# A mixture-of-experts trunk on one core: the first pair of experts of each layer started one product ahead, copied by one engine and worked in halves

## The chip, the core and the metric

The kernel runs on one core of a Trainium2 chip. A core has a matrix engine (TensorE, PE in the rows; its weight loads are the rows PEld), a vector engine (DVE), a scalar engine (ScalarE, ACT), GpSimd (POOL), a queue engine that issues most transfers (SyncE, SP), and 16 DMA engines that move data between the memory of the chip and the core's on-chip memory. TensorE writes its products to accumulation banks, from which ScalarE and the vector engine read them.

The metric is the device time of one execution in microseconds. A kernel is timed in several runs, and the median counts. One further execution is recorded by the hardware profiler; its rows are quoted below.

## What is computed

Two decoder layers over 256 tokens of width 1024. Each layer is a token mixer (a gated linear recurrence in layer 0, a stick-breaking attention in layer 1, both beside a cross-attention into a memory) and a two-level mixture of experts, each followed by a residual and a layer norm. The change is in the mixture of experts:

```python
def hier_moe(x, w_group, b_group, w_router, b_router, w_gate, w_up, w_down):
    probs_g = jax.nn.softmax((xf @ w_group + b_group), axis=-1)
    p_top, g_idx = lax.top_k(probs_g, 1)
    logits_e = (xf @ w_router + b_router).reshape(T, N_GROUPS, EXPERTS_PER_GROUP)
    in_group = jnp.take_along_axis(logits_e, g_idx[:, :, None], axis=1)[:, 0]
    probs_in = jax.nn.softmax(in_group, axis=-1)
    w_top, e_local = lax.top_k(probs_in, TOP_K_IN_GROUP)
    w_top = w_top / jnp.sum(w_top, axis=-1, keepdims=True)
    ...
    h = jax.nn.silu(jnp.einsum('td,edf->tef', xf, w_gate)) * jnp.einsum('td,edf->tef', xf, w_up)
    y = jnp.einsum('tef,efd->td', h * gates[:, :, None], w_down)
```

There are 16 experts with 256 inner features each; every token goes to two of them. The products with the experts' weights are in 32-bit floats.

## The kernel before

**Tiling.** The experts are worked in eight pairs, p = 0 to 7. Each expert has 64 slots for tokens, so that a pair fills 128 columns of inputs. For a pair, the rows of the tokens in its slots are brought together (features in partitions, tile `xg` for even and `ex` for odd p), multiplied with the gate and up weights into one accumulation bank `gu` (the two experts in the two halves of the partitions; gate columns 0 to 255, up columns 256 to 511), put through Silu and multiplied (`h`, lines L871 to L876), transposed (`ht`, copied to `hT`, L895 to L900), and multiplied with the down weights into two banks `po` of 512 output columns each (L908 to L925). A gate and up step over one block of 128 features is two products of 64 rows by 512 columns, one for each expert; eight such blocks k = 0 to 7 make the sum. A program product shows as two records of half its work, and those of the two experts of a pair run side by side.

**Weights.** All weights stream through SyncE's queue as tiles of 1 MB, `w` in the rows (line L94). Six tiles belong to a pair: four for gate and up, two for down. A ring of buffers holds them; a tile's transfer starts when its buffer is free and when the transfer three tiles before it has landed. `stream.done` gives buffers back.

**The head of a mixture.** At the end of the mixer (`mixer_end`, L937 to L1092) the second half of the tokens (t = 1) is normed while its features are transposed into the router's input: `turn_in` (L561 to L567) makes four transposes into one bank `zt` and lets ScalarE copy it to `sT`; `logits` (L569 to L574) multiplies with the router's weights. From the ranks come one-hot matrices of the slots: `P0` for the first pair, `P1` for all. The first pair's rows are gathered by products with `P0` (`gather_first`, L635 to L645, into `xgp`), the later pairs' by a DMA with computed indices: `indices` (L653 to L670) makes 16 small products of one column (tile `idx`) and starts the fetches of pairs 1 and 2 on GpSimd. `first_rows` (L647 to L651) applies the norm's scale and shift to the gathered rows, blocks 0 to 3 by ScalarE and 4 to 7 by the vector engine. `gates` (L696 to L728) works out the gate values on the vector engine and, with two products `tot`, the largest count of tokens of an expert.

**The order.** Up to the end of `mixer_end`'s routing, the order on DVE, PE and ACT is that of the code (`manual_schedule`). Behind it (L1069 onward: `moe.indices`, `moe.first_rows`, `moe.run`) instructions in `pin(...)` keep the order of the code on their engine, and a scheduler places the rest.

**The first pair in `run`** (L803 to L934): `gu(0, range(4))` multiplies blocks 0 to 3, then `gates` and `turn(0)` (two small products `ptp` that turn the gates into the order of slots), then blocks 4 to 7. Silu and the product with up follow in two parts of 128 features (`parts`), the two transposes `ht`, the first `po` bank (L913), the eight transposes `xgp` of the next pair's rows (L791), and the second `po` bank; pair 1's products come next. `hr` is the copy of `po` on its way out.

## Time and profile before

| | |
|---|---|
| median of three runs | 525.6 us (524.14 to 529.12) |
| the profiled execution, its own time | 526.96 us |
| its span in the trace | 525.3 us |
| busy: PE | 491.1 us (93%) |
| busy: PEld | 326.7 us (62%) |
| busy: DVE | 300.2 us (57%) |
| busy: ACT | 229.6 us (44%) |
| busy: POOL | 62.9 us (12%) |
| moved by DMA | 161.61 MB, mean 308 GB/s |

The two mixtures of experts lie at about 166 to 278 us (layer 0) and 408 to 512 us (layer 1). A row of the timeline has the start in us from the span's start, the duration in us, the engine, the line of the program, the operation, the tiles (out<-in), the shapes, and `x` with the number of instructions that were merged into the row; in brackets stands how long the engine was idle before it, and what released it. A q behind an engine's name is its sequencer or queue. Ends of TensorE's products are modelled, and a merged row lasts to the end of its last instruction, which can overlap the next row.

### The profile page before, as it was taken

The numbers are of one execution on the slowest core, as the hardware profiler recorded it, in microseconds if no ns is written. First come the engines' busy times: TensorE is split into PE (matmuls) and PEld (weight loads), VectorE is DVE, ScalarE is ACT, GpSimd is POOL, SyncE is SP. The second block draws the span as 40 slices with busy tenths as digits, with TensorE's granted clock in tenths as the row PEclk, the third lists the DMA queues.
The fourth block names the chain that finished last, engine by engine and source line by source line (L and its number), as shares of the span: only waits on it lengthen the run. The fifth ranks groups of instructions, "written<-read, shape, count | busy, mean of one in ns | idle before, by whom it ended". The sixth has DMA issues, their size and how long they took to land. (4 is left out here: it accounts for less than half of the span.)

```text
span 525.3 us, 9096 instructions
## 1 busy us (share of the span) xinstructions
PE 491.1 (93%) x3534; PEld 326.7 (62%) x3534; DVE 300.2 (57%) x682; ACT 229.6 (44%) x471; POOL 62.9 (12%) x78
## 2 busy tenths in 40 slices
PE   4999999999999999999797999998998899999992
PEld 4998898788996333333236889877687333333431
DVE  4668876867758622233338698677445842233547
ACT  4845446684445222333017566668423232222322
POOL 1100000002132111112011500000010121111201
PEclk9999999999999999999898999999998999999997
DMA  8999834447888999999999763242999799999922
GB/s 270 407 404 404 345 103 160 161 156 326 299 332 321 384 403 384 394 385 407 409 379 395 271 252 143 100 160 99 381 365 364 288 382 419 414 422 409 412 119 81
DMA packets 28439, 161.61 MB, mean 308 GB/s; under 512 B 5239, under 2 KB 5623, under 8 KB 11363
## 3 DMA queue, kind: packets, MB, share of 16 engines
q1 hardware_dynamic: 20736, 140.76, 68.3%
q0 software_dynamic: 4752, 10.94, 5.4%
q10 hardware_dynamic: 2902, 9.26, 4.8%
q8 instruction: 30, 0.49, 0.4%
q14 instruction: 19, 0.16, 0.1%
HBM read 158.92 MB, written 13.64 MB: 329 GB/s over the span
## 5 line engine op out<-in xcount | busy, mean ns | idle before, releaser
L820 PE MATMUL gu<-w,ex 128*64 128x512 f32 x256 | 62.9, 609 | 3.4 <-DMA w<-in_w_all_dram 2.3
L820 PE MATMUL gu<-w,xg 128*64 128x512 f32 x256 | 60.8, 601 | 0.1
L913 PE MATMUL po<-w,hT 128*64 128x512 f32 (+1 forms) x272 | 58.4, 570 | 0.1
L913 PEld LDWEIGHTS po<-w,hT 128*64 128x64 f32 x272 | 18.8, 136 | 34.0 <-issue 27.3
L820 PEld LDWEIGHTS gu<-w,ex 128*64 128x64 f32 x256 | 17.2, 137 | 34.8 <-issue 26.1
L820 PEld LDWEIGHTS gu<-w,xg 128*64 128x64 f32 x256 | 16.4, 136 | 26.5 <-issue 24.6
L920 DVE COPY hr<-po 128x512 f32<-128x512 f32 x10 | 6.9, 692 | 43.1 <-PE po L913 43.0
L629 ACT ACTIVATE xg<-xgp,lnT 128x128 f32<-128x128 f32 x32 | 13.5, 457 | 25.6 <-PE xgp L791 22.4
L918 DVE TENSOR_TENSOR hl<-po,hl 128x512 fp32r<-128x512 f32 (+1 forms) x14 | 8.5, 615 | 26.5 <-ACT hl L917 25.5
L627 DVE TENSOR_SCALAR xg<-xgp,lnT 128x128 f32<-128x128 f32 x32 | 12.4, 408 | 19.0 <-ACT xg L629 15.7
L629 ACT ACTIVATE ex<-xgp,lnT 128x128 f32<-128x128 f32 x32 | 14.3, 458 | 19.3 <-PE xgp L791 19.0
L627 DVE TENSOR_SCALAR ex<-xgp,lnT 128x128 f32<-128x128 f32 x32 | 13.1, 410 | 15.1 <-ACT ex L629 13.9
L900 ACT ACTIVATE hT<-ht 128x256 f32<-128x256 f32 (+1 forms) x18 | 6.5, 360 | 34.4 <-PE ht L899 34.3
L873 ACT ACTIVATE h<-gu 128x256 f32<-128x256 f32 (+1 forms) x18 | 6.3, 360 | 34.3 <-PE gu L820 34.3
L234 DVE TENSOR_TENSOR wo<-w,wo 128x512 fp32r<-128x512 f32 x20 | 13.7, 727 | 10.8 <-ACT wo L226 10.8
L760 POOL DMA_INDIRECT hd<-hr,own x10 | 10.1, 1014 | 81.2 <-DVE gsl L780 76.3
L673 POOL DMA_INDIRECT zg<-zd,idx x14 | 14.6, 1041 | 43.2 <-PE xgp L791 25.1
L791 PEld LDWEIGHTS xgp<-cst,zg 128*128 128x128 f32 x112 | 12.0, 141 | 11.4 <-PE gu L820 7.3
L1291 POOL TENSOR_TENSOR rms<-rms,neghalf 128x2 f32<-128x2 f32 x6 | 4.1, 699 | 111.6 <-ACT sq L1287 99.4
L384 POOL PARTITION_BROADCAST gbm<-gbm x4 | 5.3, 1398 | 94.2 <-DMA gbm<-in_ln_dram 85.5
L226 ACT ACTIVATE wo<-w 128x512 fp32r<-128x512 f32 x20 | 11.5, 628 | 9.8 <-PE wo L472 8.2
L917 ACT ACTIVATE hl<-po 128x512 fp32r<-128x512 f32 (+1 forms) x14 | 7.5, 537 | 18.4 <-PE po L913 18.4
(462 smaller groups left out, 1357.7 us busy)
## 6 DMA issues: line engine op xcount, KB each, us to landing
w<-in_w_all_dram SPq DMA_DIRECT2D x131, 1024.0 KB
hd<-in_w_all_dram ACTq DMA_DIRECT2D x2, 2560.0 KB
w<-in_w_all_dram SPq DMA_DIRECT2D x6, 256.0 KB
x_tok<-in_x_tok_dram ACTq DMA_DIRECT2D x1, 1024.0 KB
zd<-z ACTq DMA_DIRECT2D x2, 512.0 KB
gbo<-in_ln_dram ACTq DMA_DIRECT2D x1, 1024.0 KB
out_dram<-z SPq DMA_DIRECT2D x4, 256.0 KB
w<-in_w_all_dram SPq DMA_DIRECT2D x1, 512.0 KB
```

The costliest lines, as they stand in the source:

```text
L226: self.last_hi = nc.scalar.activation(p[:, 0, s], src[:, s], AF.Copy, scale=1.0 if scale is None else scale).ins
L234: nc.vector.tensor_sub(p[:, 1, s], src[:, s], p[:, 0, s])
L627: ins = nc.vector.tensor_scalar(xg[:, kk], ps, g, b, op0=ALU.mult, op1=ALU.add)
L629: nc.scalar.activation(xg[:, kk], ps, AF.Identity, scale=g, bias=b)
L673: nc.gpsimd.indirect_dma_start(out=self.zg[:, p % 2], out_offset=None, in_=self.zd, in_offset=bass.IndirectOffsetOnAxis(ap=self.idx[:, p:p ...
L760: pin(nc.gpsimd.indirect_dma_start(out=self.hd, out_offset=bass.IndirectOffsetOnAxis(ap=self.own[:, p:p + 1], axis=0), in_=src, in_offset= ...
L791: pin(nc.tensor.transpose(ps[:, k], self.zg[:, p % 2, (4 * hk + k) * P:(4 * hk + k + 1) * P], ident))
L820: pin(nc.tensor.matmul(gus[p][c * 64:(c + 1) * 64], xgs[p][:, kk, c * CAP:(c + 1) * CAP], ws[p][2 * kh + c][0][:, k * 512:(k + 1) * 512], ...
L913: pin(nc.tensor.matmul(po[c * 64:(c + 1) * 64], hT[:, f, c * 64:(c + 1) * 64], ws[p][4 + c][0][:, f * D + s.start:f * D + s.stop], start=( ...
L917: self.hl_last = nc.scalar.activation(hl[:, 0, s], po, AF.Copy).ins
L918: pin(nc.vector.tensor_sub(hl[:, 1, s], po, hl[:, 0, s]))
L920: nc.vector.tensor_copy(hr[:, p % 2, s], po)
```

## The change

1. `turn_in`: for t = 1 and the second half of the features (hk = 1) the copy to `sT` is made in two parts of 256 columns, each after two of the four transposes.
2. `first_rows`: all eight blocks of the first pair are made by ScalarE (`features(..., 0)`).
3. `indices` is called in `run`, behind the first block's products `gu(0, range(1))`, and its 16 products are pinned there; blocks 1 to 3 and `gates` follow. The two products `tot` are not pinned.
4. Pair 0's gate and up columns are put in another order in the bank: first gate and up of inner features 0 to 127, then gate and up of 128 to 255. Blocks 0 to 3 are multiplied in whole width; blocks 4 to 7 once for the first half of 256 columns and then once for the second, which makes 16 products of 256 columns from 8 of 512. Silu and the product with up read the halves.
5. Pair 0's down products: for the first 128 inner features into both `po` banks as soon as the first part of `hT` is there, then the transpose of the second part, then the second 128 features for the first bank, the next pair's eight transposes, and the second 128 features for the second bank.

The same code serves both layers.

```diff
--- before.py
+++ after.py
@@ -562,9 +562,12 @@
 
             ps = bank(f"zt{self.l}", tag="y", shape=(P, 4, P))
             sT = self.sT[t, hk] = self.tmp.tile([P, 4, P], F32, tag="sT", name=f"sT{self.l}{t}", bufs=2)
+
+            n = 2 if t == hk == 1 else 4
             for k in range(4):
                 nc.tensor.transpose(ps[:, k], s[:, t, (4 * hk + k) * P:(4 * hk + k + 1) * P], ident)
-            nc.scalar.activation(sT, ps, AF.Copy)
+                if k % n == n - 1:
+                    nc.scalar.activation(sT[:, k + 1 - n:k + 1], ps[:, k + 1 - n:k + 1], AF.Copy)
 
         def logits(self, t, hk):
             if hk == 0:
@@ -647,7 +650,7 @@
         def first_rows(self):
             xg = self.work.tile([P, NK, P], F32, tag="xg", name=f"xg{self.l}")
             for k in range(NK):
-                self.features(xg, self.first[k // 4][:, k % 4], k, k // 4)
+                self.features(xg, self.first[k // 4][:, k % 4], k, 0)
             return xg
 
         def indices(self):
@@ -658,8 +661,8 @@
             ps = bank(f"idx{l}", tag="m", shape=(P, 8))
             for p in range(8):
                 for t in range(NT):
-                    nc.tensor.matmul(ps[:, p:p + 1], self.P1f[:, t, p * P:(p + 1) * P], tokb[:, t:t + 1], start=(t == 0),
-                                     stop=(t == 1))
+                    pin(nc.tensor.matmul(ps[:, p:p + 1], self.P1f[:, t, p * P:(p + 1) * P], tokb[:, t:t + 1],
+                                         start=(t == 0), stop=(t == 1)))
 
 
             pin(nc.vector.tensor_scalar(self.idx[:, 0:3], ps[:, 0:3], float(T), T - 1.0, op0=ALU.add, op1=ALU.min))
@@ -809,7 +812,7 @@
 
             quarters = [slice(0, 512), slice(512, 768), slice(768, D)]
 
-            def gu(p, ks):
+            def gu(p, ks, part=slice(0, 512)):
 
                 if p not in ws:
                     ws[p] = [stream.get() for _ in range(6)]
@@ -817,10 +820,13 @@
                 for kk in ks:
                     kh, k = kk // 4, kk % 4
                     for c in range(2):
-                        pin(nc.tensor.matmul(gus[p][c * 64:(c + 1) * 64], xgs[p][:, kk, c * CAP:(c + 1) * CAP],
-                                            ws[p][2 * kh + c][0][:, k * 512:(k + 1) * 512], start=(kk == 0),
-                                            stop=(kk == NK - 1)))
-                    if k == 3:
+                        w = ws[p][2 * kh + c][0][:, k * 512:(k + 1) * 512]
+                        if p == 0:
+                            w = w.rearrange("p (g h n) -> p h g n", g=2, h=2)
+                            w = w if part.stop - part.start == 512 else w[:, part.start // 256]
+                        pin(nc.tensor.matmul(gus[p][c * 64:(c + 1) * 64, part], xgs[p][:, kk, c * CAP:(c + 1) * CAP],
+                                            w, start=(kk == 0), stop=(kk == NK - 1), skip_group_check=(p == 0)))
+                    if k == 3 and part.stop == 512:
                         stream.done(ws[p][2 * kh][1], ws[p][2 * kh + 1][1])
 
             def combine(p, t, s):
@@ -835,10 +841,13 @@
 
             for p in range(8):
                 if p == 0:
-                    gu(0, range(4))
+                    gu(0, range(1))
+                    self.indices()
+                    gu(0, range(1, 4))
                     self.gates()
                     self.turn(0)
-                    gu(0, range(4, 8))
+                    for j in range(2):
+                        gu(0, range(4, 8), slice(256 * j, 256 * j + 256))
                     self.ex = slots.tile([P, 2, D], F32, tag="ex", name=f"ex{l}")
                 else:
 
@@ -869,11 +878,14 @@
                 h = pool.tile([P, 256], F32, name=f"h{l}")
 
                 parts = [slice(0, 256)] if p else [slice(0, P), slice(P, 256)]
-                for c in parts:
-                    nc.scalar.activation(h[:, c], gus[p][:, c], AF.Silu)
-                for c in parts:
-                    pin(nc.vector.scalar_tensor_tensor(h[:, c], gus[p][:, 256 + c.start:256 + c.stop],
-                                                       self.gsl[:, p:p + 1], h[:, c], op0=ALU.mult, op1=ALU.mult))
+
+                g = [c.start * (1 if p else 2) for c in parts]
+                n = 256 // len(parts)
+                for c, o in zip(parts, g):
+                    nc.scalar.activation(h[:, c], gus[p][:, o:o + n], AF.Silu)
+                for c, o in zip(parts, g):
+                    pin(nc.vector.scalar_tensor_tensor(h[:, c], gus[p][:, o + n:o + 2 * n], self.gsl[:, p:p + 1], h[:, c],
+                                                       op0=ALU.mult, op1=ALU.mult))
                 if p == 0:
                     self.turn(1)
                     yield None
@@ -892,12 +904,23 @@
                 if p == 7:
                     beyond(pool, self.pool, self.ex, l, base, self.x1, self.most, self.late, y)
                 hT = pool.tile([P, 2, P], F32, name=f"hT{l}")
+
+                def down(po, s, fs):
+                    for f in fs:
+                        for c in range(2):
+                            pin(nc.tensor.matmul(po[c * 64:(c + 1) * 64], hT[:, f, c * 64:(c + 1) * 64],
+                                                ws[p][4 + c][0][:, f * D + s.start:f * D + s.stop],
+                                                start=(f == 0), stop=(f == 1)))
+                pos = [bank(f"po{l}", tag="m") for _ in half] if p == 0 else []
                 for c in parts:
                     fs = slice(c.start // P, c.stop // P)
                     ht = bank(f"ht{l}", tag="m", shape=(P, 2, P))
                     for f in range(fs.start, fs.stop):
                         pin(nc.tensor.transpose(ht[:, f], h[:, f * P:(f + 1) * P], ident))
                     nc.scalar.activation(hT[:, fs], ht[:, fs], AF.Copy)
+                    if p == 0 and fs.start == 0:
+                        for po, s in zip(pos, half):
+                            down(po, s, (0,))
                 if 0 < p < 7:
                     gu(p + 1, range(2, 3))
                 if p > AWAY:
@@ -907,12 +930,8 @@
                     hl = keep.tile([P, 2, D], F32R, tag="v", name=f"hl{l}")
                 for hf, s in enumerate(half if p < 7 else quarters):
                     n = s.stop - s.start
-                    po = bank(f"po{l}", tag="m")[:, 0:n]
-                    for f in range(2):
-                        for c in range(2):
-                            pin(nc.tensor.matmul(po[c * 64:(c + 1) * 64], hT[:, f, c * 64:(c + 1) * 64],
-                                                ws[p][4 + c][0][:, f * D + s.start:f * D + s.stop],
-                                                start=(f == 0), stop=(f == 1)))
+                    po = pos[hf] if p == 0 else bank(f"po{l}", tag="m")[:, 0:n]
+                    down(po, s, (1,) if p == 0 else range(2))
                     if p >= AWAY:
                         self.hl_last = nc.scalar.activation(hl[:, 0, s], po, AF.Copy).ins
                         pin(nc.vector.tensor_sub(hl[:, 1, s], po, hl[:, 0, s]))
@@ -1066,7 +1085,6 @@
         tmp.release()
         work = tc.alloc_tile_pool(name=f"moe{l}", bufs=1, side="right", reuse_waits="tile")
         moe.start(work)
-        moe.indices()
         xg = moe.first_rows()
         gb = rows(2 * l, f"m{l}")
         for p in moe.run(xg):
```

Where instructions stand before and after is shown at three places of layer 1. A row has the line, the operation, out<-in and the shape; `[waits ...]` names the engines' counters and DMA queues that the instruction waits for (PE_49 TensorE's, Activation_49 ScalarE's, DVE_49 the vector engine's, DMAHW and DMASW the transfers').

The first place is the last block of `turn_in` on TensorE, with the logits behind it. Before, four transposes in a row and four logit products behind one copy:

```order
L566 MATMUL zt_4220<-cst,z_3007 128x128 [waits DVE_49]
L566 MATMUL zt_4220<-cst,z_3007 128x128 x3
L573 MATMUL lg_4212<-rw,sT_4221 128x20 [waits Activation_49]
L573 MATMUL lg_4212<-rw,sT_4221 128x20 x3
L644 MATMUL xgp_4255<-P_4097,z_3007 128x128 [waits DVE_49,PE_49]
```

After, on the same engine:

```order
L568 MATMUL zt_4229<-cst,z_3016 128x128 [waits DVE_49]
L568 MATMUL zt_4229<-cst,z_3016 128x128
L568 MATMUL zt_4229<-cst,z_3016 128x128 [waits Activation_49]
L568 MATMUL zt_4229<-cst,z_3016 128x128
L576 MATMUL lg_4221<-rw,sT_4230 128x20 x2
L576 MATMUL lg_4221<-rw,sT_4230 128x20 [waits Activation_49]
L576 MATMUL lg_4221<-rw,sT_4230 128x20
L647 MATMUL xgp_4265<-P_4106,z_3016 128x128 [waits DVE_49,PE_49]
```

The third transpose now waits for ScalarE, which copies the first half of the bank, and the third logit product waits for ScalarE's second copy.

The second place is the first gate and up products on TensorE (`gu`). Before, they stand behind all the index products, and what waits for a feature block is `xg`:

```order
L661 LDWEIGHTS P_4096
L661 MATMUL idx_4305<-tokb,P_4096 128x1
L820 MATMUL gu_4345<-w_4056,xg_4332 64x512 [waits DMAHW2_49,Activation_49]
L820 MATMUL gu_4345<-w_4058,xg_4332 64x512 [waits DMAHW1_49]
L820 MATMUL gu_4345<-w_4056,xg_4332 64x512 [waits Activation_49]
L820 MATMUL gu_4345<-w_4058,xg_4332 64x512
```

After, the first block's two products are ahead of the index products:

```order
L827 MATMUL gu_4327<-w_4065,xg_4314 64x512 [waits DMAHW2_49,DVE_49,Activation_49]
L827 MATMUL gu_4327<-w_4067,xg_4314 64x512 [waits DMAHW1_49]
L664 LDWEIGHTS P_4105
L664 MATMUL idx_4331<-tokb,P_4105 128x1
L664 LDWEIGHTS P_4105 [waits DVE_49]
L664 MATMUL idx_4331<-tokb,P_4105 128x1
```

The 16 index products, with the two of `tot` among them in this layer, moved from ahead of the first block to between the first and the second. In layer 0 the two of `tot` stand further on, between the third and the fifth block.

The third place is the end of the first pair, on TensorE and on ScalarE. TensorE before, from the transposes of `h` to the second `po` bank:

```order
L899 MATMUL ht_4418<-cst,h_4402 128x128 [waits DVE_49]
L899 MATMUL ht_4421<-cst,h_4402 128x128 [waits DVE_49,PE_49]
L913 MATMUL po_4424<-w_3755,hT_4417 64x512 [waits Activation_49]
L913 MATMUL po_4424<-w_3833,hT_4417 64x512 [waits DMAHW3_49]
L913 MATMUL po_4424<-w_3755,hT_4417 64x512 [waits Activation_49]
L913 MATMUL po_4424<-w_3833,hT_4417 64x512
L791 MATMUL xgp_4430<-cst,zg_4303 128x128 [waits DMASW1_49,DVE_49,PE_49]
L791 MATMUL xgp_4430<-cst,zg_4303 128x128 x3
L791 MATMUL xgp_4439<-cst,zg_4303 128x128 [waits PE_49]
L791 MATMUL xgp_4439<-cst,zg_4303 128x128 x3
L913 MATMUL po_4451<-w_3755,hT_4417 64x512 [waits PE_49]
L913 MATMUL po_4451<-w_3833,hT_4417 64x512
```

TensorE after, from just behind the first transpose of `h`; one more product of the last line's kind follows:

```order
L911 MATMUL po_4436<-w_3764,hT_4435 64x512 [waits Activation_49]
L911 MATMUL po_4436<-w_3842,hT_4435 64x512 [waits DMAHW3_49]
L911 MATMUL po_4437<-w_3764,hT_4435 64x512 [waits PE_49]
L911 MATMUL po_4437<-w_3842,hT_4435 64x512
L919 MATMUL ht_4445<-cst,h_4420 128x128 [waits DVE_49,PE_49]
L911 MATMUL po_4436<-w_3764,hT_4435 64x512 [waits Activation_49]
L911 MATMUL po_4436<-w_3842,hT_4435 64x512
L794 MATMUL xgp_4451<-cst,zg_4313 128x128 [waits DMASW1_49,PE_49]
L794 MATMUL xgp_4451<-cst,zg_4313 128x128 x3
L794 MATMUL xgp_4460<-cst,zg_4313 128x128 [waits PE_49]
L794 MATMUL xgp_4460<-cst,zg_4313 128x128 x3
L911 MATMUL po_4437<-w_3764,hT_4435 64x512
```

Both banks' products for the first 128 features moved ahead of the second transpose, and the products for the second 128 features stand on both sides of the next pair's transposes. ScalarE before, from the first Silu to the copy of `po`:

```order
L873 ACTIVATE h_4402<-gu_4345 128x128 [waits PE_49]
L873 ACTIVATE h_4402<-gu_4345 128x128
L900 ACTIVATE hT_4417<-ht_4418 128x128 [waits PE_49]
L900 ACTIVATE hT_4417<-ht_4421 128x128 [waits PE_49]
L922 ACTIVATE hr_4416<-po_4424 128x512 [waits DMAHW2_49,DMAHW4_49,DVE_49,PE_49]
```

ScalarE after:

```order
L885 ACTIVATE h_4420<-gu_4327 128x128 [waits PE_49]
L885 ACTIVATE h_4420<-gu_4327 128x128
L920 ACTIVATE hT_4435<-ht_4438 128x128 [waits PE_49]
L920 ACTIVATE hT_4435<-ht_4445 128x128 [waits PE_49]
L941 ACTIVATE hr_4434<-po_4436 128x512 [waits DMAHW2_49,DMAHW4_49,DVE_49,PE_49]
```

The order of ScalarE's instructions is the same. The count of TensorE for which the first Silu waits is that of the last product of pair 0's gate and up in both: after, the last of the second half's.

## Rows read from the trace of the kernel before

**Rows 1.** Stretches: from:to, length, busy of PE, PEld, DVE, ACT, POOL; clock; DMA

```profile
201.00:250.00 49.00, 49.00 (x248) 17.46 (x244) 15.02 (x36) 13.72 (x31) 8.06 (x8) 1.00 1.00 400
250.35:254.79 4.44, 1.06 (x4) 0.19 (x3) 1.05 (x3) 0.38 (x1) 0.99 (x1) 1.00 1.02 409
254.93:258.34 3.41, 3.41 (x7) 0.57 (x5) 1.98 (x2) 0.00 (x0) 0.00 (x0) 0.50 1.02 417
...
430.00:505.00 75.00, 75.00 (x370) 27.05 (x368) 25.67 (x60) 19.44 (x44) 11.09 (x11) 1.00 0.98 402
```

**Rows 2.** TensorE's waits: us in total, times, longest us

```profile
PE gu L820 <- DMA w<-in_w_all_dram: 2.3, 1, 2.3
```

**Rows 3.** Timeline of TensorE, layer 0, last pair's first products

```profile
251.45 1.04 PE L820 MATMUL gu<-w,ex 128*64 128x512 f32 x2 [1.08 <-DVE h L875]
254.79 3.57 PE L820 MATMUL gu<-w,ex 128*64 128x512 f32 x6 [2.30 <-DMA w<-in_w_all_dram]
258.29 1.21 PE L828 MATMUL y<-hl,PT 128*128 128x512 f32 x4
```

**Rows 4.** Timeline, layer 1, the last transposed block and the logits

```profile
399.57 0.66 PE L566 MATMUL zt<-cst,z 128*128 128x128 f32 x4 [0.42 <-DVE z L399]
400.26 0.60 ACT L567 ACTIVATE sT<-zt 128x512 f32<-128x512 f32 x1 [2.04 <-PE zt L566]
...
400.92 1.20 PE L573 MATMUL lg<-rw,sT 128*128 128x20 f32 x8 [0.69 <-ACT sT L567]
...
401.95 3.54 PE L644 MATMUL xgp<-P,z 128*128 128x128 f32 x16
```

**Rows 5.** Timeline, layer 1, up to the first gate and up products

```profile
406.24 2.02 PE L644 MATMUL xgp<-P,z 128*128 128x128 f32 x16 [0.71 <-DVE dl L690]
...
408.30 1.50 ACT L629 ACTIVATE xg<-xgp,lnT 128x128 f32<-128x128 f32 x4 [1.41 <-PE xgp L644]
...
409.18 0.33 PE L661 MATMUL idx<-tokb,P 128*128 128x1 bf16 x7 [0.25 <-DVE P L614]
...
409.44 3.65 PE L820 MATMUL gu<-w,xg 128*64 128x512 f32 x16
```

**Rows 6.** Timeline, layer 0, the first pair's products

```profile
165.92 0.45 PEld L661 LDWEIGHTS <-P 128*128 128x128 bf16 x15
...
166.58 3.65 PE L820 MATMUL gu<-w,xg 128*64 128x512 f32 x16
...
170.32 3.65 PE L820 MATMUL gu<-w,xg 128*64 128x512 f32 x16
```

**Rows 7.** Timeline, layer 1, the end of the first pair

```profile
416.90 0.45 ACT L873 ACTIVATE h<-gu 128x128 f32<-128x128 f32 x2 [5.80 <-PE gu L820]
417.38 0.61 DVE L875 SCALAR_TENSOR_TENSOR h<-gu,gsl,h 128x128 f32<-128x128 f32 x2 [1.25 <-ACT h L873]
...
417.79 0.65 PE L899 MATMUL ht<-cst,h 128*128 128x128 f32 x2 [0.80 <-DVE h L875]
...
418.48 1.94 PE L913 MATMUL po<-w,hT 128*64 128x512 f32 x8
...
420.35 1.09 PE L791 MATMUL xgp<-cst,zg 128*128 128x128 f32 x8
...
421.37 1.94 PE L913 MATMUL po<-w,hT 128*64 128x512 f32 x8
...
423.14 4.46 PE L820 MATMUL gu<-w,ex 128*64 128x512 f32 x20
```

**Rows 8.** Timeline of SyncE's queue, layer 0, behind the first pair's products

```profile
176.77 0.33 SPq L94 DMA_DIRECT2D w<-in_w_all_dram  x1
```

**Rows 9.** Timeline, layer 0, products and copies of 256 columns

```profile
163.72 0.28 PE L262 MATMUL mv1p<-mv,mem 128*128 128x256 f32 x1
...
163.84 0.28 PE L263 MATMUL mv1p<-mv,mem 128*128 128x256 f32 x1
...
163.92 0.74 ACT L1340 ACTIVATE memv<-mv1p 128x256 f32<-128x256 f32 x2 [1.03 <-PE mv1p L264]
```

## The prediction

> **What bounds the kernel now.** I read the busy times by stretches first, because the share over the whole span mixes stages. In both expert stages TensorE is busy all the time once the first pair is through: 49.00 of 49.00 us in layer 0 and 75.00 of 75.00 us in layer 1, the DMA engines at 1.00 and 0.98 beside it [rows 1]. So two limits lie close together, and the next view, TensorE's waits and its timeline, tells which one closes each stage. In layer 0 it is the weights: the list of waits has one wait of the gate and up products for weights, 2.30 us [rows 2], and the timeline puts it at the end, in the last pair [rows 3]. TensorE runs out of work at 250.37 (251.45 less the 1.08 us it then waited for the vector engine's h), gets one column half of a product, and stands from 252.49 to 254.79 until a weight tile lands. [...] In layer 1 no such wait follows: there every microsecond that TensorE loses in the first pair is a microsecond of the result. This decides how the change is priced: layer 1's first pair counts in full, layer 0's only as far as its delay outlasts the wait at 254.79.
>
> **The change part by part, in layer 1.** The profiled execution's own time is 526.96 us with a span of 525.3; the median of the three runs is 525.6. The sum is a difference made inside that span, and I put it on the median.
>
> T1, the last transposed block copied in halves. Now the four transposes start at 399.57, ScalarE copies at 400.26 for 0.60, the logits start at 400.92 and the next products at 401.95 [rows 4]. With halves the first copy can start two transposes earlier, about 0.22 us (399.57 to 400.26 less the pipeline, four transposes in all), and takes 0.37 (two copies of 256 columns took 0.74 [rows 9]). But the order shows the third transpose waiting for ScalarE's first copy, and so the steps stand in a row: copy to about 400.41, transposes to 400.93, second copy to 401.30, and the last two logits to 401.88. That is 0.07 less than 401.95; I take -0.1. Bounds: -0.4 if copy and transposes overlapped, +0.3 if each of the two handovers more costs 0.2.
>
> T2, one product ahead of the indices. The first product starts at 409.44 [rows 5], behind index matmuls that themselves wait for the vector engine's one-hot P (0.25 us, the last piece of several). Its own needs are met earlier: ScalarE's first feature block starts at 408.30 and takes 0.375 plus some 0.08 until TensorE sees it (four take 1.50 [rows 5]), so it can start at about 408.75: -0.69. Now the index and token-count matmuls lay in that wait and cost nothing; behind the first product they stand between products with nothing to hide them. A product follows the other every 0.43 us (four take 1.94 with the tail of the last, some 0.22 [rows 7]). By that an insertion of two small matmuls costs 0.30: the eight products from 166.58 are through at 170.02, and behind the two the next start at 170.32 [rows 6]. Each further one costs 0.030 (15 weight loads in 0.45 [rows 6]). So 18 cost 0.30 + 16 x 0.030 = 0.78, and T2 is +0.09; I take +0.1. Bounds: -0.69 if the insertion were free, +0.4 if it falls into two groups. The products do not then wait for features: ScalarE makes all eight blocks at 0.375 each while the two products of a block take 0.86. The vector engine is 1.36 us freer, but TensorE did not wait for its gates: the products run without a pause from 409.44 for 3.65 us [rows 5], and the gate values are needed only behind them. So edit 2 is worth nothing on the path; if the cover were gone, it could give back at most those 1.36 us to the index fetch, which is not waited for either.
>
> T3, sixteen products of 256 columns for eight of 512. The columns are the same. 256-column products followed each other every 0.12 us with a load of 0.19 beside them (163.72 to 163.84 [rows 9]), so short products need not show their loads. I take +0.05; bounds 0 and +0.16 (0.02 for each of eight).
>
> T4, the order of the down products. The order makes the first Silu wait for the last product of the second half, as before it waited for the last of all. So its start, and that of the down products 1.6 us behind it (416.90 to 418.48 [rows 7]), do not move. Ahead of the next pair's first product now stand four down products (418.48 to 420.35, 1.87), eight transposes (1.02) and four down products (1.77), in all 4.66 us to 423.14 [rows 7]. After, it is four products (1.87), then the transpose of the second half of h, its copy by ScalarE and the handover back, then two products (0.86), the transposes (1.02), two products (0.91). The transpose is queued behind the four products on the same engine, so nothing hides its chain, which now takes 0.69 (417.79 to 418.48 [rows 7]); what is queued behind it on TensorE is the rest of the pair. Sum 5.35, and T4 is +0.69. Bounds +0.3 (transpose and copy alone at their shortest) and +0.9.
>
> [...]
>
> Layer 1: -0.1 + 0.1 + 0.05 + 0.69 = **+0.74 us**.
>
> **In layer 0** the start at 166.58 stays, since it hangs on ScalarE's first block. The 16 index matmuls cost 0.30 + 14 x 0.030 = 0.72, the two of the count 0.30 in their own place, T3 0.05, T4 0.69: 1.76 us later at TensorE. The weights don't follow: the next tile of this stretch is issued by SyncE at 176.77 [rows 8], while TensorE is done with the pair's gate and up tiles at 173.97 (170.32 and 3.65 [rows 6]), so the ring has 2.8 us to give. TensorE then comes to the last pair 1.76 us later, at 252.1, and waits 0.54 instead of 2.30. The delay is swallowed whole; without that cover it would be +1.76.
>
> What goes with the wait is the point I had to choose. The fall to half clock stood behind idle stretches of 1.08 and 2.30 us, and 3.41 us at half speed cost 1.71 [rows 1]. With 1.08 and 0.54 left, I take it that the clock stays up. An idle piece of 0.80 us ahead of 417.79 [rows 7] was followed by no fall, and the stretch that was has twice the idle time that is left. From 254.79 on TensorE waits for no weights any more [rows 2], so these 1.71 us come off the end of the stage. Forecast: 525.6 + 0.74 - 1.71 = **524.6 us** (526.0 by the profiled execution's own time).
>
> **The rivals.**
>
> The fall stays: TensorE is still idle for 1.6 of 2.7 us before 254.79, and the records can't tell how much less is enough. Then only the sum stands: 525.6 + 0.74 = 526.3 us.
>
> On the slower side, a further fall in layer 1's first pair. The kernel before has one at 401.95, where sixteen small products take 3.54 us [rows 4] against 2.02 for the same sixteen at 406.24 [rows 5]; it stands behind short waits close together (0.42 and 0.69 us [rows 4]). The change sets a wait of 0.69 us 1.9 us behind the one of 0.80 us at 417.79. If the clock falls there, 1.71 us are lost in a stretch that counts in full: 526.3 + 1.7 = 528.0 us. It decides from the point where the granted clock between 418 and 424 is under 1. Against it: ahead of it lie 7 us of products almost without a gap.
>
> The halves do overlap, so that the change does what its form says: the Silu of the first half runs beside the second half's products and the down products start 0.87 us sooner (two products of 512 columns' time). Then 524.6 - 0.9 = 523.7 us. Against it stand the waits in the order.
>
> Layer 0's delay is not absorbed, because SyncE's queue moves with it (the transfers behind a late release start later, and DMA at 1.00 [rows 1] can't catch up): 526.3 + 1.8 = 528.1 us. Against it stand the 2.8 us of slack.
>
> **How the numbers follow.** Forecast 0.42 (own range 523.8 to 525.0: T4's bounds and half of T2's); the fall stays 0.33; a further fall 0.10; the halves overlap 0.08; not absorbed 0.07. The range takes in the bounds: at the low end -0.4 - 0.69 + 0 + 0.3 = -0.8 with the fall gone, 523.1; at the high end 0.3 + 0.4 + 0.16 + 0.9 = +1.76 with the fall still there, 527.4. Outside lie the two cases at 528, 0.17 together. A measurement of this kernel can tell about 1% from no change, which is 5.3 us, 520.3 and 530.9. No case reaches either; I leave 0.03 on each side for what I did not see, and 0.94 between.
>
> **What would show it.** In layer 1: the first product about 0.7 us ahead of 409.44 but the second half of the gate products no earlier than 413.1; the first Silu at the same distance behind the last product; a wait of TensorE near 0.7 us between the fourth and fifth down product, and some 5.3 us from the first of them to the next pair. In layer 0: the wait for weights in the last pair at about 0.5 us and a granted clock of 1.00 behind it. The forecast is wrong if that wait keeps its 2.3 us, if the clock is at half behind 254.8, or if TensorE waits for weights in layer 1.

## The result, and the profile after

The changed kernel takes 529.5 us in the median, the kernel before 525.92 us, over 20 executions of each. The ratio is 1.0069, with a 95% interval from 1.0045 to 1.0093: 3.6 us slower (2.4 to 4.9). The forecast was 524.6 us, with 523.1 to 527.4 as its range. Single executions of one kernel scatter by several microseconds (519.08 to 530.39 us for the kernel before), which matters below: a profiled execution is one draw. The ratios, and the means below, leave out the executions that lie more than 1.5% above the fastest of their kernel.

The profiled execution of the changed kernel has a span of 528.3 us. First, TensorE in layer 1 from the last transposed block to the second pair:

```profile
399.43 0.44 PE L568 MATMUL zt<-cst,z 128*128 128x128 f32 x2 [0.42 <-DVE z L399]
400.34 0.44 PE L568 MATMUL zt<-cst,z 128*128 128x128 f32 x2 [0.47 <-ACT sT L570]
400.62 1.68 PE L576 MATMUL lg<-rw,sT 128*128 128x20 f32 x8
402.13 3.76 PE L647 MATMUL xgp<-P,z 128*128 128x128 f32 x16
...
406.64 3.75 PE L647 MATMUL xgp<-P,z 128*128 128x128 f32 x16 [0.71 <-DVE dl L693]
410.94 1.08 PE L827 MATMUL gu<-w,xg 128*64 128x512 f32 x4 [0.55 <-ACT xg L632]
411.95 0.38 PE L664 MATMUL idx<-tokb,P 128*128 128x1 bf16 x9
...
412.48 2.80 PE L827 MATMUL gu<-w,xg 128*64 128x512 f32 x12
415.21 0.22 PE L776 MATMUL ptp<-G,P 128*128 128x48 bf16 x2
415.36 3.67 PE L827 MATMUL gu<-w,xg 128*64 128x256 f32 x32
...
419.99 0.33 PE L919 MATMUL ht<-cst,h 128*128 128x128 f32 x1 [0.80 <-DVE h L887]
420.69 1.94 PE L911 MATMUL po<-w,hT 128*64 128x512 f32 x8 [0.37 <-ACT hT L920]
422.55 0.33 PE L919 MATMUL ht<-cst,h 128*128 128x128 f32 x1
423.25 1.08 PE L911 MATMUL po<-w,hT 128*64 128x512 f32 x4 [0.37 <-ACT hT L920]
424.26 1.09 PE L794 MATMUL xgp<-cst,zg 128*128 128x128 f32 x8
425.29 1.08 PE L911 MATMUL po<-w,hT 128*64 128x512 f32 x4
426.19 4.46 PE L827 MATMUL gu<-w,ex 128*64 128x512 f32 x20
```

The last rows, from 420.69, are T4: from the first down product to the next pair 5.50 us (420.69 to 426.19), against 4.66 in [rows 7], and the waits for hT at both transposes. The rows from 410.94 to 415.21 are T2: 4.27 us from the first product to the small ones, where it was 3.59.

Layer 0's first pair shows the same steps with a larger T2; its counts stand in a place of their own:

```profile
167.85 1.08 PE L827 MATMUL gu<-w,xg 128*64 128x512 f32 x4 [0.55 <-ACT xg L632]
168.86 0.55 PE L664 MATMUL idx<-tokb,P 128*128 128x1 bf16 x16
...
171.21 0.18 PE L726 MATMUL tot<-Ab,onesb 128*128 128x16 bf16 x1
...
172.33 0.18 PE L726 MATMUL tot<-Ab,onesb 128*128 128x16 bf16 x1
172.37 0.21 PE L776 MATMUL ptp<-G,P 128*128 128x48 bf16 x2
```

From 167.85 to 172.37 are 4.52 us. Before, the small products stood 3.59 us behind the first product of [rows 6] (166.58 to 170.17), so it is 0.93 more:

```profile
170.17 0.22 PE L773 MATMUL ptp<-G,P 128*128 128x48 bf16 x2
```

With T3 and T4 that makes 1.8 us later in layer 0, as the forecast had it (from the first product to the next pair's first 15.49 us, where it was 13.70).

What the forecast rested on looks different. TensorE's timeline at layer 0's last pair, where [rows 3] had the wait for weights, and TensorE's whole list of waits from 225 to 281:

```profile
253.26 1.89 PE L827 MATMUL gu<-w,ex 128*64 128x512 f32 x8
255.07 1.20 PE L834 MATMUL y<-hl,PT 128*128 128x512 f32 x4
```

```profile
PE ht L919 <- DVEq L489: 2.4, 1, 2.4
```

There is no wait for weights any more and no fall of the clock there, but there is a wait of 2.4 us further on, ahead of the last pair's transposes (270.03), and the clock is at half in other places. The stretches of the changed kernel, in the columns of [rows 1]:

```profile
253.00:255.00 2.00, 2.00 (x10) 0.43 (x6) 1.14 (x2) 0.38 (x1) 0.59 (x1) 1.00 0.99 410
270.90:274.30 3.40, 3.40 (x11) 0.96 (x11) 0.00 (x0) 0.02 (x1) 0.00 (x0) 0.51 0.98 369
400.84:411.08 10.24, 8.98 (x43) 8.56 (x45) 6.47 (x31) 2.46 (x5) 0.33 (x1) 0.51 0.86 298
411.08:428.00 16.92, 15.38 (x106) 6.60 (x106) 9.98 (x29) 6.90 (x17) 3.23 (x3) 1.00 0.74 287
```

From 411.08 to 428.00, layer 1's first pair, the clock is at 1.00, so the rival of a further fall there did not come about. In layer 1's routing head TensorE's granted clock is at half (0.51, the third row) for 10.2 us in this execution; in the profiled execution of the kernel before it was 3.4 us (401.95 in [rows 4] lies in it). So the first theory to test was a **clock theory**: the change puts more short waits into that head, and the clock does the rest (ahead of the fall stand waits of 0.42 and 0.47 us here, of 0.42 and 0.69 us in the kernel before; that such waits bring it was the author's guess). Its rival was a **delay theory**: the steps are what the trace shows, about 0.9 us in layer 1 and 1.8 us in layer 0, and layer 0's delay is not swallowed.

### The profile page after: what moved, and what is told of

Its sections match the earlier page's. It is cut to its first block, busy times and chain, and to the rows that moved or that the text cites. A ratio compares the mean times of both kernels' runs of the same rounds, so it can differ in the third digit from the quotient of the medians.

```text
span 528.3 us, 9162 instructions
## 1 busy us (share of the span) xinstructions
PE 494.2 (94%) x3566; PEld 332.5 (63%) x3566; DVE 298.3 (56%) x674; ACT 232.7 (44%) x481; POOL 62.9 (12%) x78
## 5 line engine op out<-in xcount | busy, mean ns | idle before, releaser
L827 PE MATMUL gu<-w,xg 128*64 128x512 f32 (+1 forms) x288 | 61.5, 554 | 1.1 <-ACT xg L632 1.1
L911 PE MATMUL po<-w,hT 128*64 128x512 f32 (+1 forms) x272 | 60.2, 582 | 1.5 <-ACT hT L920 1.5
L827 PE MATMUL gu<-w,ex 128*64 128x512 f32 x256 | 60.2, 599 | 0.0
L827 PEld LDWEIGHTS gu<-w,xg 128*64 128x64 f32 x288 | 18.4, 136 | 24.8 <-issue 19.4
L632 ACT ACTIVATE xg<-xgp,lnT 128x128 f32<-128x128 f32 x40 | 16.3, 462 | 25.6 <-PE xgp L794 20.7
L632 ACT ACTIVATE ex<-xgp,lnT 128x128 f32<-128x128 f32 x32 | 14.3, 458 | 19.3 <-PE xgp L794 19.0
L630 DVE TENSOR_SCALAR xg<-xgp,lnT 128x128 f32<-128x128 f32 x24 | 9.7, 410 | 17.5 <-ACT xg L632 16.9
```

The costliest lines, as they stand in the source:

```text
L630: ins = nc.vector.tensor_scalar(xg[:, kk], ps, g, b, op0=ALU.mult, op1=ALU.add)
L632: nc.scalar.activation(xg[:, kk], ps, AF.Identity, scale=g, bias=b)
L827: pin(nc.tensor.matmul(gus[p][c * 64:(c + 1) * 64, part], xgs[p][:, kk, c * CAP:(c + 1) * CAP], w, start=(kk == 0), stop=(kk == NK - 1), s ...
L911: pin(nc.tensor.matmul(po[c * 64:(c + 1) * 64], hT[:, f, c * 64:(c + 1) * 64], ws[p][4 + c][0][:, f * D + s.start:f * D + s.stop], start=( ...
```

## The experiments

Each result is the ratio to the kernel before, measured beside it, with its 95% interval. Beside it stands the mean time lost at half speed, worked out for each timed execution that the comparison counts as one minus its mean granted clock, times its span. It includes the end of the program, where TensorE has little to do. Over 112 executions of the kernel before it is 9.7 us, over 26 of the changed kernel 10.6 us. So half speed as a whole differs by 0.9 us between them, not by the 5 us that the two profiled executions suggest (14.3 and 8.9 us lost).

**One edit undone at a time**

```diff
 u1  - n = 2 if t == hk == 1 else 4
     + n = 4
 u3  - gu(0, range(1)); self.indices(); gu(0, range(1, 4))
     + gu(0, range(4))                       # and moe.indices() back ahead of moe.first_rows()
 u4  - for j in range(2): gu(0, range(4, 8), slice(256 * j, 256 * j + 256))
     + gu(0, range(4, 8))
 u5  - down(po, s, (0,)) for both banks behind the first transpose, (1,) later
     + down(po, s, range(2)) for each bank behind both transposes
```

> The changed kernel with edit 1 undone: the last transposed block of each layer is copied to sT in one piece of 512 columns again; the other four edits stay. Clock theory (most of the 3.6 us is TensorE at half speed in layer 1's routing head, brought there by the two handovers between TensorE and ScalarE that edit 1 adds): at least 1.7 us faster than the changed kernel, some 527.5 us, and fewer microseconds at granted clock 0.50 between 400 and 412. Work theory (the 3.6 us are the steps themselves, down order 0.84, indices 0.7, copy 0.3 and so on in each layer): 0.3 us faster, some 529.2 us, and the clock there unchanged.

> The changed kernel with edit 3 undone: the index products stand ahead of the first gate and up product again. Clock theory: the stretch 406 to 412 has less idle time on TensorE with them there, so the half-speed windows in layer 1's head become fewer: 1 to 2 us faster than the changed kernel. Work theory: the first product starts 0.7 us later and the 0.7 us of small products between the first two blocks go: no difference over 0.2 us, 529.4 us.

> The changed kernel with the second half of pair 0's gate and up products in whole width again (8 products of 512 columns instead of 16 of 256; the order of the columns in the bank stays). Both theories: no difference over 0.2 us, 529.4 us, since the second half took 3.61 us from its first product to the next small one, against 3.58 before.

> The changed kernel with edit 5 undone: both transposes of pair 0's h stand ahead of the down products again, each bank's products in one go. Both theories: 0.84 us faster than the changed kernel by layer 1 (5.50 against 4.66 us from the first down product to the next pair), nothing by layer 0, whose delay ends at the transfer that its last pair waits for: 528.7 us. The clock theory leaves the rest of the 3.6 us standing here; if more than 1.5 us go, this edit has a second effect.

| undone | ratio to before | lost at half speed |
|---|---|---|
| nothing (the changed kernel) | 1.0069 (1.0045 to 1.0093) | 10.5 us |
| edit 1, u1 | 1.0020 (0.9974 to 1.0066) | 9.9 us |
| edit 3, u3 | 1.0085 (1.0046 to 1.0124) | 12.7 us |
| edit 4, u4 | 1.0070 (1.0037 to 1.0103) | 10.4 us |
| edit 5, u5 | 1.0008 (0.9971 to 1.0046) | 10.0 us |

Edit 5 is the one whose undoing takes most away: 0.6 points, 3.2 us, with an uncertainty of about 2.4. Undoing edit 1 takes 0.5 points, 2.6 us, with an uncertainty of 2.7, so the two are not told apart. u5's trace shows what goes in each layer, 4.66 us from the first down product to the next pair again:

```profile
418.62 1.94 PE L911 MATMUL po<-w,hT 128*64 128x512 f32 x8
...
423.28 2.31 PE L827 MATMUL gu<-w,ex 128*64 128x512 f32 x9
```

That is 0.84 us in layer 1, and 0.84 in layer 0 if that layer's delay counts; expected was 0.84 in all. u4 came out as expected. u1 can't be told from either theory, although its trace has only 3.4 us at half speed in layer 1's head. u3 did not get faster, though 0.93 us of layer 0's T2 is gone from its trace; it lost 2 us more at half speed than the changed kernel, and why is not settled. No run undoes edit 2 alone. So undoing single edits did not decide between the theories.

**Two undone, and edit 1 alone**

u15 has the edits of u1 and u5 together; t1 puts edit 1 alone into the kernel before.

> The changed kernel with edits 1 and 5 undone, so that the earlier first product, the first rows by ScalarE and the halves of gate and up remain. By the steps read so far (indices +0.05, halves +0.02 in layer 1) it should be the kernel before within 0.3 us, and its half-speed time that of the kernel before. If the earlier first product is itself what brings the half-speed time, it stays 1.5 us or more above the kernel before.

> The kernel before with edit 1 alone. By the steps: from the last transposes to the first gathering 0.3 us longer, 526.2 us. Clock theory: more half-speed time in the heads besides, 1 to 2 us more, 527.2 to 528.2 us.

u15 has a ratio of 1.0009 (0.9964 to 1.0054) and lost 9.7 us, t1 has 1.0012 (0.9975 to 1.0049) and lost 10.5. Neither differs from the kernel before by what can be measured, but up to 2.8 and 2.6 us of loss lie inside the intervals, and with them what either theory expected. The traces say more about the clock. Layer 1's head is at half speed in all ten that have no idle transposes there (next part): for 6.8 to 13.6 us in the six with edit 1, 9.1 on average, and for 3.4 to 13.7 us in the four without it, 8.6 on average. They show no sign that edit 1 brings the fall there.

**Idle transposes in layer 1's routing head**

```diff
+        def warm(self, n):
+            if not hasattr(self, "fill"):
+                self.fill = bank(f"fill{self.l}", tag="m", shape=(P, 4, P))
+            for i in range(n):
+                nc.tensor.transpose(self.fill[:, i % 4], ident, ident)
...
                 moe.logits(1, 0)
+                moe.warm(3)
                 moe.count(0)
+                moe.warm(3)
...
+                moe.warm(4)              # fA: 4 between the halves of the copy, then 2
                 moe.logits(1, 1)
...
+                moe.warm(5)
                 moe.gather_first(s, 1)
+                moe.warm(4)
```

> The changed kernel with 21 idle transposes of the identity (0.11 us each, into a bank that nothing reads) put on TensorE into the waits of layer 1's routing head, 398 to 411: ahead of the slot count, between the two halves of the copy, ahead of the logits, and on both sides of the second gathering. They compute nothing of the result. Clock theory: TensorE does not fall to half speed there any more; the 3.4 us that half speed costs in this kernel's profiled head come back in part, and the kernel is 2.5 to 3.5 us faster than the changed kernel, about 526.5 us. Work theory: nothing is gained, and what of the fillers does not fit into the waits is added: 529.5 to 530.5 us.

> The kernel before with 19 such idle transposes in the same waits of layer 1's head. Clock theory: the one half-speed stretch that its profile shows there (1.7 us lost) goes: 1 to 1.7 us faster than the kernel before, and then it beats both kernels. Work theory: no gain, at most 0.5 us slower.

> The filled kernel before once more, beside the two kernels above on the same chip, as what they are compared with: 524.2 us, half-speed time as low as before (6.4 us lost on average against 10.3 of the kernel before).

In the profiled executions of fA and of the first fB the head is at full clock throughout:

```profile
394.00:406.00 12.00, 11.73 (x103) 8.76 (x102) 9.79 (x49) 6.41 (x13) 0.56 (x1) 1.00 0.87 324
```

```profile
400.00:409.00 9.00, 8.36 (x84) 7.27 (x82) 8.01 (x36) 3.66 (x8) 0.56 (x1) 1.00 0.93 326
```

The first row is the filled changed kernel, the second the filled kernel before. In the profiled execution of fB_again the head fell all the same, for 6.8 us, so the fillers make the fall rarer (it is there in ten of ten traces without them and in two of seven with them) and don't exclude it. The time lost at half speed went down by about 3 us in both: to 7.4 us in fA, to 6.4 us in fB and 7.4 in fB_again. The filled kernel before came to 0.9988 (0.9945 to 1.0032) and 0.9940 (0.9902 to 0.9978), the second clear of the kernel before; the medians are 524.15 us beside 526.94, and 525.21 beside 525.67. With fC2 below it has the lowest medians. fA stands at 1.0042 (1.0004 to 1.0081), 1.4 us less than the changed kernel's first ratio, which is not clear of noise. Its mean of 526.64 us lies near the 526.5 that the clock theory gave and not in the work theory's 529.5 to 530.5, and fB's median is lower too, so the fillers seem to help both kernels, and the work theory was wrong in expecting nothing of them. But fA's mean is 2.4 us above the 524.25 of the 22 executions of fB and fB_again on the same chip, with a 95% interval from 0.7 to 4.1 (worked out from the scatter of the executions). **A gap between the two kernels stays when most falls in the head are taken out of both.** The clock theory falls as the explanation of most of the loss; a smaller part is inside the interval.

These two traces also give T1 at full clock, which none before had. The filled changed kernel, and then the filled kernel before, from the transposes to the gathering:

```profile
394.66 0.38 PE L568 MATMUL zt<-cst,z 128*128 128x128 f32 x2
394.88 0.60 PE L579 MATMUL fill<-cst 128*128 128x128 f32 x4
395.52 0.44 PE L568 MATMUL zt<-cst,z 128*128 128x128 f32 x2
395.79 0.38 PE L579 MATMUL fill<-cst 128*128 128x128 f32 x2
396.01 1.04 PE L585 MATMUL lg<-rw,sT 128*128 128x20 f32 x8
396.90 2.03 PE L656 MATMUL xgp<-P,z 128*128 128x128 f32 x16
```

```profile
400.27 0.66 PE L566 MATMUL zt<-cst,z 128*128 128x128 f32 x4
400.76 0.60 PE L574 MATMUL fill<-cst 128*128 128x128 f32 x4
401.61 1.07 PE L580 MATMUL lg<-rw,sT 128*128 128x20 f32 x8 [0.25 <-ACT sT L567]
402.53 2.03 PE L651 MATMUL xgp<-P,z 128*128 128x128 f32 x16
```

2.24 us against 2.26: with the fillers in, T1 is worth nothing at full clock. No trace without them has this stretch at full clock.

**The edits in one layer only**

r0 has fB's fillers and r1 those of fA, and each edit stands behind `if l == 0` or `if l == 1`.

> All five edits in layer 0 alone, layer 1 as in the kernel before; the idle transposes stand in layer 1's head as in the filled kernel before, so that the clock there does not blur the comparison. By the steps layer 0's first pair ends 1.8 us later (0.94 indices and counts, 0.02 halves, 0.85 down order). Theory that the delay passes through (the 2.30 us wait for weights in the last pair was there in one execution and is not in the usual one): 1.8 us slower than the filled kernel before, about 526 us. Theory of the prediction (the delay is swallowed by that wait): equal to it, 524.2 us.

> All five edits in layer 1 alone, layer 0 as in the kernel before, with the idle transposes in layer 1's head. Both theories: 0.9 us slower than the filled kernel before (0.05 indices, 0.02 halves, 0.85 down order), about 525.1 us. If the whole difference between the two filled kernels, some 3 us, lay in layer 1, it would be 527 us.

r0 came to 1.0009 (0.9978 to 1.0041) and r1 to 0.9999 (0.9959 to 1.0038), where fB_again, measured with them, had 0.9940. Set against all 22 executions of fB and fB_again, r0 is 2.9 us slower (1.2 to 4.5) and r1 2.0 us (0.1 to 3.9). For layer 0 the 1.8 us of the delay theory lie inside, no loss at all lies outside; for layer 1 the 0.9 us lie inside, and so would 3. The split between the layers is not settled by these two.

**A known delay in layer 0**

```diff
                 if p == 0:
                     gu(0, range(4))
+                    if l == 0:
+                        idle = bank("idle", tag="m", shape=(P, 4, P))
+                        for i in range(32):
+                            pin(nc.tensor.transpose(idle[:, i % 4], ident, ident))
```

> The kernel before with 32 idle transposes of the identity (0.11 us each, 3.5 us, computing nothing of the result) put on TensorE in layer 0's first pair, between its fourth and fifth block. Theory that layer 0's delay passes through: 3.5 us slower than the kernel before, about 529.5 us. Theory of the prediction (the wait for weights at the end of layer 0 swallows the first 2.3 us): 1.2 us slower, about 527 us.

It came to 1.0087 (1.0051 to 1.0124), 530.08 us beside 525.79: 4.6 us slower, 2.7 to 6.5. The delay itself is 3.60 us (from the first gate product to the small ones 7.19 us, against 3.59). That it passes through lies inside the interval, and that 2.3 us of it are swallowed (1.2 us left) lies outside. **Delay theory holds for this.** Some of the 4.6 us can be clock: d32 lost 10.7 us at half speed, the kernel before beside it 9.4. The trace shows the way the delay takes. GpSimd's last fetch of rows (`zg<-hd`) is issued behind the vector engine's h of pair 6; the vector engine waits for it, and the last pair's h, which TensorE's transposes `ht` need, is queued behind that on the vector engine. The first gate product of layer 0 and GpSimd's fetch, in t1 (layer 0's first pair as before but for the copy), the changed kernel and d32:

```profile
166.38 3.65 PE L822 MATMUL gu<-w,xg 128*64 128x512 f32 x16
...
251.15 0.99 POOL L754 DMA_INDIRECT zg<-hd,back  x1 [4.75 <-DVE h L877]
...
261.48 1.23 DVE L802 TENSOR_TENSOR zg<-zg,second 128x1024 f32<-128x1024 f32 x1 [1.07 <-DMA zg<-hd,back]
...
265.41 0.41 PE L901 MATMUL ht<-cst,h 128*128 128x128 f32 x2 [1.05 <-DVEq L489]
```

```profile
253.89 0.48 DVE L887 SCALAR_TENSOR_TENSOR h<-gu,gsl,h 128x256 f32<-128x256 f32 x1 [0.23 <-ACT h L885]
...
254.41 0.98 POOL L755 DMA_INDIRECT zg<-hd,back  x1 [4.20 <-DMA w<-in_w_all_dram]
...
266.13 2.05 DVE L803 TENSOR_TENSOR zg<-zg,second 128x1024 f32<-128x1024 f32 x1 [2.46 <-DMA zg<-hd,back]
```

```profile
167.04 3.65 PE L820 MATMUL gu<-w,xg 128*64 128x512 f32 x16 [0.17 <-ACT xg L629]
...
255.40 0.99 POOL L752 DMA_INDIRECT zg<-hd,back  x1 [4.53 <-DVE h L879]
...
268.06 1.62 DVE L800 TENSOR_TENSOR zg<-zg,second 128x1024 f32<-128x1024 f32 x1 [2.92 <-DMA zg<-hd,back]
```

From the first product to the issue of the fetch it is 84.77 us in t1, 86.56 in the changed kernel (its first product is at 167.85 above) and 88.36 in d32: 1.79 and 3.59 us more, layer 0's step and the known delay (3.60) to a hundredth. The changed kernel's row names a weight transfer as the releaser, but there too the fetch follows the end of pair 6's h by 0.04 us. From pair 1's first product to the fetch it is 71.06 to 71.08 us in all 17 traces. So the fetch hangs on TensorE, and every trace tells what a step in the first pair does to the end of layer 0. From layer 0's first product, in us:

| traces | layer 0's first pair | to the fetch | to the last pair's transposes |
|---|---|---|---|
| t1, fB, fB_again, fC, fC2 | without T2, T3 and T4 | 84.76 to 84.78 | 99.03 to 101.25, mean 100.24 |
| u5, u15 | without T4 | 85.72, 85.73 | 100.64, 101.20 |
| u3 | without T2 | 85.63 | 100.95 |
| after, after_again, r0, fA, u1, u4 | with T2 and T4 | 86.54 to 86.57 | 100.92 to 102.30, mean 101.66 |
| d32 | the known delay | 88.36 | 104.50 |

The time that the fetch then takes differs by execution, hence the scatter of the last column. Its mean moves by 1.4 us for the change's 1.8, and d32 lies 4.3 us above it for the known 3.6: the delay reaches the end of layer 0 and is not swallowed. Two traces are left out. The kernel before's own one has 105.03 us, with the wait for weights and the fall in it; r1 has 103.90, because its first pair in layer 0 took 4.4 us longer, with a wait of 2.96 us for pair 1's rows.

**The boundary between the layers, and the changed kernel again**

fC put 20 idle transposes ahead of the next layer's first transposes (`turn_in(0, range(8))` at the boundary), fC2 put 22 there with `pin`.

> The filled kernel before with 20 more idle transposes ahead of the first transposes of the boundary between the layers, where TensorE waits 2.8 us for the vector engine and every profile so far shows a fall to half speed (1.7 us lost). Clock theory: the fall goes, and 1 to 1.7 us with it: 522.5 to 523.2 us. If the stage there is bound by the vector engine and the weights rather than by TensorE, the half-speed time falls by 1.7 us but the time stays.

> The filled kernel before with 22 idle transposes at the boundary between the layers, now held behind layer 0's last products, where the run before it had them among these products (they added 2 us there and left the wait at 2.60 us). Clock theory: the fall behind that wait goes and the kernel is 1 to 1.7 us faster than the filled kernel before, about 523 us. If the vector engine and the weights bound that stage, the half-speed time falls and the time stays at 524.5 us.

> The changed kernel once more, unchanged, beside the two above, for its half-speed time and the wait for weights at the end of layer 0 in another execution. Delay theory: 2.7 us slower than the kernel before by its steps (0.9 in layer 1, 1.8 in layer 0), no wait for weights in layer 0's last pair. Theory of the prediction: within 1 us of the kernel before wherever the half-speed times are alike.

fC does not test what it was meant to: the scheduler set its fillers among layer 0's last products, and the wait stayed at 2.60 us. It came to 1.0012 (0.9978 to 1.0047). In fC2 they fill the wait, and the clock holds:

```profile
273.80 2.56 PE L1428 MATMUL z2t<-cst 128*128 128x128 f32 x22
276.68 1.11 PE L1396 MATMUL z2t<-cst,z 128*128 128x128 f32 x8 [0.32 <-DVE z L1392]
```

```profile
274.00:290.00 16.00, 14.37 (x107) 12.59 (x106) 15.42 (x40) 12.27 (x25) 6.16 (x10) 1.00 0.91 332
```

It lost 5.5 us at half speed, the least of all, and yet came to 0.9994 (0.9955 to 1.0034), no better than fB. In that stage the vector engine is busy for 15.42 of 16 us, which would explain it. But fC2's mean (524.40 us, on another chip) is 0.15 us above that of the 22 executions, give or take 1.7, so a gain of 1 to 1.5 us is not excluded. after_again came to 1.0051 (1.0017 to 1.0085), 2.7 us, with 10.7 us lost at half speed: the 2.7 us of the steps.

## Why the prediction was wrong, point by point

**T1** was taken as -0.1 us; at full clock and with the fillers in it is 0.0. In the two profiled executions, partly at half clock, the stretch took 2.70 us in the changed kernel against 2.38. t1 shows no loss from that (1.0012), but can't exclude one of 0.3 us.

**T2** in layer 1 was +0.1. The first product came 0.63 us sooner behind the end of the gathering (0.55 us after it, the wait at 410.94; 1.18 before, 408.26 to 409.44 in [rows 5]), and the block of products behind it took 0.68 longer: +0.05. In layer 0 it was 1.02, and 0.93 was measured. That the index fetch "is not waited for either" held in 16 of the 17 traces; r1 has the wait of 2.96 us. **T3** was +0.05, and 0.02 was measured (3.61 for 3.59 us).

**T4** was +0.69 us, 0.84 was measured. The chain of transpose, copy and handover cost 0.70 us, as priced (422.55 to 423.25). The 0.15 on top lie in the two products behind it: 1.01 us from their start to the next transposes (423.25 to 424.26), where 0.86 was taken. That the halves would not overlap held: the Silus start at 419.11, behind the last of the 32 records from 415.36 (3.67 us), and the vector engine's h (419.59) when both Silus, 0.45 us, are done:

```profile
419.11 0.45 ACT L885 ACTIVATE h<-gu 128x128 f32<-128x128 f32 x2 [4.48 <-PE gu L827]
419.59 0.61 DVE L887 SCALAR_TENSOR_TENSOR h<-gu,gsl,h 128x128 f32<-128x128 f32 x2 [1.27 <-ACT h L885]
```

From the last product to the Silus it is 0.08 us, and from these to h 0.03 us. The first of these waits stands in the kernel's order, where the first Silu waits for the last product of the second half; no run here lets two engines at one bank together, so whether the halves could overlap without it was not shown.

So layer 1's sum was nearly right: 0.74 forecast, 0.91 by the traces.

**Layer 0's delay** was the step that failed. Its size was right (1.76 forecast, 1.79 measured); that "the delay is swallowed whole" was wrong: it was booked at nothing, and the traces and d32 show it passing through. The cover was one wait for weights of 2.30 us in the one profiled execution of the kernel before, in [rows 2, 3]. Of the 17 traces that now exist, 15 have no such wait at all, and u15 has one of 0.4 us. The usual end of layer 0 is not the weights but the row fetch and the vector engine's work behind it, and that chain moves with TensorE, as d32 and the table showed. The stated rival "layer 0's delay is not absorbed" was the nearest case, at 528.1 us with a chance of 0.07; its reason was SyncE's queue, and what the traces show is GpSimd's fetch.

**The fall of the clock** was the other. The forecast took 1.71 us off the median because the fall behind 254.79 would go. The changed kernel's trace has neither the fall nor the wait, but none of the other 15 traces, with or without the edits, has a fall there either: that stretch is at 1.00 in 16 of 17. A loss of one profiled execution was taken off a median of executions that, by these traces, mostly did not have it. So nothing was gained: what the steps cost, 0.9 and 1.8 us, is what is left, and their 2.7 us lie within both intervals measured for the changed kernel, 2.4 to 4.9 and 0.9 to 4.5 us. What remains above them, up to 0.9 us, is as large as the difference in time lost at half speed, but whether the change causes that was not shown. None of the signs named as showing the forecast wrong came about (the wait is gone, the clock behind it is at 1.00, layer 1 has no wait for weights): they all looked at this one place.

## What to carry to other kernels

Before a delay is booked as hidden in a wait, ask whether that wait is there in every execution: here a wait for a weight transfer stood in one trace of 17 at its full length, and a fetch that is issued behind the late engine's products hid nothing. Work moved out of a wait into a row of products cost its full length (0.68 us for 0.63 gained), and halves of a bank brought no overlap where the next engine waits for the whole bank (the Silus start 0.08 us behind the last product of the second half); the added transpose chain was then a plain loss of 0.7 us. Where single executions scatter by several microseconds, put a known delay in and measure that.

## What the runs showed of the hardware

In layer 1's head TensorE's granted clock was 0.50 for a part of it in all ten traces without fillers there; in the two profiled executions the fall stands behind waits of 0.42 and 0.69 us (before) and of 0.42 and 0.47 us (after). How long it lasts differs between executions of the same program: 10.2 and 6.8 us in two traces of the changed kernel. Of the seven traces with idle transposes in these waits five have no fall there, and two (fB_again and r0) have one of 6.8 us. The fillers brought the mean time lost at half speed down by about 3 us, and the kernel before became 1.3 us faster on average (524.25 over 22 executions against 525.53 over 112, some on other chips), less than the time that was no longer lost. How much of the difference the fillers themselves cost was not measured.
